# Projections over all rows in four blocks of 448 columns instead of three of 512 and one of 256, and retention values in two blocks of 384 instead of 512 and 256

## The chip, the cores and the metric

One core of a Trainium2 chip runs the whole program as a single launch. The metric is the time of one execution in microseconds on the device: the median over runs. The times before are 3032.01, 3036.05 and 3033.46 us.

## The reference

A sequence of 512 tokens, 2048 features wide, goes through one hybrid layer (dilated attention and an HGRN2 scan, then an output projection, then a gate built from a second projection) and through two further layers (retention, differential attention and an RG-LRU, then an output projection). What the change touches:

```python
# first block, once
y = concatenate([y_att, y_hg]) @ w_out            # (512, 2048) @ (2048, 2048)
h = h + rmsnorm(y, g_post)
gate = sigmoid(h @ w_pg)                          # (512, 2048) @ (2048, 2048)
e = p_l @ w_pp                                    # (512, 256) @ (256, 2048)
h = h + rmsnorm(gate * e, g_ple)
# second block, for l in range(2)
rv = (rms_norm(x) @ w_in[l])[:, 1536:2304]        # values of 6 retention heads of 128
y = concatenate([ret_out, diff_out, lru_out]) @ w_out[l]
x = x + rms_norm(y, post_norm_g[l])
```

All of it is float32. Each product is made of three matmuls on split operands: `hi*hi`, `hi*lo` and `lo*hi`, where `hi` is the value rounded to the fp32r format of TensorE and `lo` is what is left.

## The kernel before

**Projections.** `wpiece` loads a piece of weights by one DMA on SP's queue into `raw` (two buffers), ScalarE rounds it into `whi` and VectorE subtracts to get `wlo`, each in two halves (four buffers of each, so that two pieces are ready or in use). `projT` computes rows of tokens by columns of weights: for each of 16 slices `k` of 128 features and each of the four token tiles `t` it issues three matmuls whose stationary operand is a 128x128 tile of the input (`uh`, `ul`) and whose moving operand is a row of weights `cw` columns wide. With `cw=512` a piece holds two slices `k` and each `t` has a PSUM bank of its own (tile `acct`); with `cw=256` a piece holds four slices and two `t` share a bank. The callback `cb` empties a bank when its sum is complete: one `t` after the other for 512 columns, all four at the end for 256.

**Output projections.** `tok_rows` is called four times (for `w_out`, `w_pg` and `w_out_2` of both layers) and works through 2048 columns: three calls of `projT` with 512, one with 256 columns, and then a last 256 columns whose weights stay resident for all 16 slices (tile `accl`), so that the four token tiles can be finished one by one. Only when the last columns of a token tile are known can its row be normalised: `tok_rstd`, then four times `x += y * r` of 512 columns each (`SCALAR_TENSOR_TENSOR` on VectorE, tile `x`). While the last token tiles are still being multiplied, `new_rows` already transposes finished columns of `x` through a PSUM bank (tile `mb`, three banks) into the next input `uh`, `ul`. In the last layer each finished chunk is stored instead. For the gate, `ple_cols` makes `e` in column blocks: two blocks stand between the first two calls of `tok_rows`, interleaved with `new_rows` of the last two token tiles, and the other two are handed out during the second call.

**Retention.** `ret_round` runs three times per layer. Each projects `q` and `k` of two heads, rotates them (`rope`: per half, four VectorE products `rt`, one product with `C`, one addition on GpSimd), and, in rounds 0 and 2, projects values by `head_v`: four heads with `cw=512` in round 0, two with `cw=256` in round 2. The mixing of two heads (`ret_mix`) is a generator in a queue behind that of the LRU. `tick` hands out one unit of the queue each time that the projection's matmuls have earned `spacing` of credit.

**Order.** TensorE's instructions stand as they are written. The order of the other engines comes from a scheduler with priorities.

Of the kernel before, what the change touches and what calls it, by code (L numbers as in the profile page):

```python
# [17 lines left out]
P = 128  # L18
# [62 lines left out]
class Net:  # L81
# [505 lines left out]
    def head_v(self, pool, tag, wap, c0, U, h0, n, bufs=6):  # L587

        vts = []
        for h in range(0, n, 2):  # L590
            vts.append(pool.tile([P, 4, 256], F32, tag=tag, name=tag, bufs=bufs // 2))

        def vcb(t, ps):
            for h in range(n if t == 3 else 0):
                self.vts[h0 + h] = vts[h // 2][:, :, h % 2 * P:(h % 2 + 1) * P]
            for h, v in enumerate(vts):
                self.nc.scalar.activation(v[:, t, :], ps[:, h * 256:(h + 1) * 256], AF.Copy, scale=self.rc[:, t:t + 1])

        self.projT(wap, c0, U, vcb, cw=n * P)
# [188 lines left out]
    def tok_rows(self, pool, wap, gi, U, order, evac, X, fresh, before=None, more=None, at=None, src=None):  # L788
# [8 lines left out]
        V.memset(ss, EPS)  # L797
        gb = {}

        def gains(c):  # L800
            g = gb[c] = pool.tile([P, T], F32, tag="gb", name="gb", bufs=2)
            S_.dma_start(g, bass.AP(tensor=a.tensor, offset=a.offset + gi * D + c, ap=[[0, P], [1, T]]))

        def out(t, c, n, acc):
            b = c // T * T
            o = slice(c - b, c - b + n)
            i = (c + 256) // T
            ins, rest = evac(t, c, n, acc, yt[t][c // T][:, o], gb[b][:, o], ss[:, t, i:i + 1])
            if src is not None and t == 3 and i < 4:
                with self.tc.issue_after(ins.ins):  # L810
                    S_.dma_start(X[i], src[i * P:(i + 1) * P, :])
            if c == 1792:
                return rest
            rest()

        gains(0)
        for c in (0, 512, 1024):
            gains(c + 512)
            if more:
                more(c)  # L820
            self.projT(wap, c, U, lambda t, acc, c=c: out(t, c, 512, acc), range(KT) if c else order,
                       before=None if c else before)
        if more:
            more(1536)
        self.projT(wap, 1536, U, lambda t, acc: out(t, 1536, 256, acc), cw=256)
        self.drain()
        wl = []
        for i in range(0, KT, 4):
            wl.extend(self.wpiece(wap, i, 4, [1792], 256, (pool, i)))
        for t in range(4):  # L830
            acc = self.accp.tile([P, T], F32, tag="acc", name="accl")[:, 0:256]
            for i in range(KT):
                if at:
                    at(t, i)
                hi, lo = wl[i]
                uh, ul = (u[:, t * P:(t + 1) * P] for u in U[i])
                nc.tensor.matmul(acc, uh, hi, start=i == 0, stop=False)  # L837
                nc.tensor.matmul(acc, uh, lo, start=False, stop=False)  # L838
                nc.tensor.matmul(acc, ul, hi, start=False, stop=i == KT - 1)  # L839
            with self.tc.high_priority(offset=3 * BIG):  # L840
                rest = out(t, 1792, 256, acc)
                r = pool.tile([P, 2], F32, tag="r", name="r", bufs=2)
                self.tok_rstd(r[:, 1:2], r[:, 0:1], ss[:, t, :])
                rest()
                for i in ((0, 1, 2, 3) if t < 2 else (1, 2, 3, 0)):
                    x = X[t][:, i * T:(i + 1) * T]
                    V.scalar_tensor_tensor(x, yt[t][i], r[:, 1:2], x, op0=ALU.mult, op1=ALU.add)
                    fresh(t, i)

# [97 lines left out]
    def first_block(self):  # L947
# [38 lines left out]
        with tc.tile_pool(name="h1", bufs=1, reuse_waits="tile") as pool:  # L986
# [7 lines left out]

            def gated(t, c, n, acc, y, g, ss):
                ins = nc.scalar.activation(y, acc, AF.Sigmoid)
                nc.vector.tensor_tensor(y, y, es[t, c // T][:, c % T:c % T + n], op=ALU.mult)
                nc.scalar.activation(sq()[:, :n], y, AF.Square, scale=D ** -0.5, accum_out=ss)
                return ins, lambda: nc.vector.tensor_tensor(y, y, g, op=ALU.mult)

            def load(c):
                if c == 512:
                    self.tables(pool, "e", EB)
                elif c == 1024:
                    self.pT = self.load_p(pool)

            self.tok_rows(pool, A["w_out"][0], 0, U, order, self.plain(sq), X, lambda t, i: None, more=load,
                          at=self.first_half(U, X, None), src=A["x"][0])
# [12 lines left out]
            def more(c):  # L1021
                self.drain()
                if c in (512, 1024):
                    self.spacing = 6.0
                    self.add(self.ple_cols(pool, c // 512 + 1, es))

            self.tok_rows(pool, A["w_pg"][0], 1, U, range(KT), gated, X, lambda t, i: None, before, more,
                          self.first_half(U, X, self.col["pre_norm_g_2"][:, 0:16], 10))
# [4 lines left out]
    def plain(self, sq):  # L1033
        def evac(t, c, n, acc, y, g, ss):
            ins = self.nc.scalar.activation(sq()[:, :n], acc, AF.Square, scale=D ** -0.5, accum_out=ss)
            return ins, lambda: self.nc.vector.tensor_tensor(y, acc, g, op=ALU.mult)
        return evac
# [14 lines left out]
    def ple_cols(self, pool, c, es):  # L1052

        nc = self.nc
        wk = self.wpiece(self.A["w_pp"][0], 0, 2, [c * T], T)
        for t in range(4):
            ps = self.bank()
            s = slice(t * P, (t + 1) * P)
            for k in range(2):
# [3 lines left out]
                nc.tensor.matmul(ps, ul, wk[k][0], start=False, stop=k == 1)  # L1063
            es[t, c] = pool.tile([P, T], F32, tag="e", name="e", bufs=EB)
            nc.scalar.activation(es[t, c], ps, AF.Copy)
# [179 lines left out]
    def ret_round(self, pool, lp, l, r, U, C, S):  # L1245
        nc, A = self.nc, self.A
        V, S_ = nc.vector, nc.scalar
        w = A["w_in_2"][l]
        rot = self.qkv(pool, w, OFF2["rq"] + 256 * r, OFF2["rk"] + 256 * r, OFF2["rv"] + 256 * r, U, C, S, 64, 6,
                       2 * r, (4, 0, 2)[r], 6)  # L1250
        self.add(self.ret_mix(pool, lp, l, r, rot))
# [143 lines left out]
    def second_layer(self, l, U, ls8):  # L1395
# [33 lines left out]
        with tc.tile_pool(name=f"h2{l}", bufs=1, reuse_waits="tile") as pool:  # L1429
# [5 lines left out]

            def store(t, i):
                o = slice(i * T, (i + 1) * T)
                (nc.sync if i % 2 else nc.scalar).dma_start(self.out[0][t * P:(t + 1) * P, o], X[t][:, o])

            at = None if l else self.first_half(U, X, self.col["pre_norm_g_2"][:, 16:32])  # L1440
            self.tok_rows(pool, A["w_out_2"][l], 2 + l, U, order, self.plain(sq), X, store if l else lambda t, i: None,
                          at=at, src=self.xs_dram)
# [14 lines left out]
NH = 6  # L1457
EB = 8
HALF = [slice(0, T // 2), slice(T // 2, T)]
WARM = 10  # L1460
# [42 lines left out]
```

## Time and profile before

| | |
|---|---|
| median of the runs shown | 3033.46 us |
| profiled execution, its own time | 3031.51 us |
| its span, first to last instruction | 3029.7 us |
| TensorE busy | 3003.6 us, 99% of the span |
| VectorE busy | 1819.7 us, 60% |
| ScalarE busy | 1467.5 us, 48% |
| GpSimd busy | 547.1 us, 18% |
| moved by DMA | 316.25 MB, mean 104 GB/s |

The profiled execution took 1.81 us more than its span, which is what lies around the span, and 1.95 us less than the median of the runs. TensorE's instructions overlap (the next begins before the modelled end of the last), so a busy share of 99% says that there is almost always a matmul in flight; how many fit into a microsecond is read from the distance between their starts.

### The profile page before, as it was taken

What the parts mean: (1) busy time and instruction counts of PE and PEld (TensorE: products, weight loads), DVE (VectorE), ACT (ScalarE), POOL (GpSimd) and SP (SyncE); (2) the same over time, 40 slices, a digit from 0 to 9 for tenths busy, and PEclk for the clock granted to TensorE, in tenths of its full rate; (3) what the DMA queues carried; (4) which work ended last, traced back from release to release, by engine and by line L of the source; (5) the groups of instructions that cost most, each with busy time, mean ns of one, the idle gap of its engine ahead of it and who ended that gap; (6) DMA issues with size and microseconds to landing.
All of it is one profiled execution on the core that took longest, in us unless ns stands there. A gap on an engine that the chain in (4) does not pass through costs nothing. (4 is left out here: it accounts for less than half of the span.)

```text
span 3029.7 us, 40507 instructions
## 1 busy us (share of the span) xinstructions
PE 3003.6 (99%) x15118; PEld 2548.1 (84%) x15118; DVE 1819.7 (60%) x3228; ACT 1467.5 (48%) x2653; POOL 547.1 (18%) x582
## 2 busy tenths in 40 slices
PE   9999999999999999999999999999999999999998
PEld 8788888888888888889888888888988888888888
DVE  5878779557776535346766455653457664566434
ACT  6444443445556424346365544662355555446532
POOL 0546546211111000001321010110013210101000
PEclk9999999999999999999999999999999999999999
DMA  5222222333332433335332233333453322323344
GB/s 164 72 80 72 77 70 77 96 107 89 85 88 76 140 122 105 101 115 170 108 114 85 84 91 105 95 93 126 160 163 93 117 84 84 111 82 100 97 131 148
DMA packets 237878, 316.25 MB, mean 104 GB/s; under 512 B 12641, under 2 KB 179777, under 8 KB 234993
## 3 DMA queue, kind: packets, MB, share of 16 engines
q1 hardware_dynamic: 219392, 260.61, 28.0%
q0 software_dynamic: 10640, 28.92, 3.8%
q10 hardware_dynamic: 7648, 24.13, 2.4%
q8 instruction: 119, 1.95, 0.3%
q14 instruction: 79, 0.64, 0.1%
HBM read 284.25 MB, written 13.63 MB: 98 GB/s over the span
## 5 line engine op out<-in xcount | busy, mean ns | idle before, releaser
L261 DVE TENSOR_TENSOR wlo<-raw,whi 128x512 fp32r<-128x512 f32 x980 | 728.8, 754 | 741.1 <-ACT whi L260 725.2
L260 ACT ACTIVATE whi<-raw 128x512 fp32r<-128x512 f32 x980 | 604.5, 627 | 998.3 <-PE acct L321 393.0
L291 PE MATMUL acc<-uh,whi 128*128 128x512 f32 (+1 forms) x2288 | 899.1, 393 | 1.7 <-ACT whi L260 1.0
L293 PE MATMUL acc<-uh,wlo 128*128 128x512 f32 (+1 forms) x2288 | 884.5, 387 | 1.3 <-DVE wlo L261 1.3
L292 PE MATMUL acc<-ul,whi 128*128 128x512 f32 (+1 forms) x2288 | 882.6, 386 | 0.0
L319 PE MATMUL acct<-whi,uh 128*128 128x512 f32 (+1 forms) x1664 | 611.9, 368 | 3.4 <-ACT hf L534 3.4
L320 PE MATMUL acct<-wlo,uh 128*128 128x512 f32 (+1 forms) x1664 | 608.5, 366 | 0.0
L321 PE MATMUL acct<-whi,ul 128*128 128x512 f32 (+1 forms) x1664 | 608.5, 366 | 0.0
L293 PEld LDWEIGHTS acc<-uh,wlo 128*128 128x128 f32 x2288 | 430.1, 188 | 91.7 <-DVE wlo L261 3.1
L291 PEld LDWEIGHTS acc<-uh,whi 128*128 128x128 f32 x2288 | 430.7, 188 | 81.6 <-ACT whi L260 1.2
L292 PEld LDWEIGHTS acc<-ul,whi 128*128 128x128 f32 x2288 | 431.2, 188 | 79.7 <-issue 0.2
L319 PEld LDWEIGHTS acct<-whi,uh 128*128 128x128 f32 x1664 | 314.6, 189 | 54.1 <-ACT hf L534 4.2
L321 PEld LDWEIGHTS acct<-whi,ul 128*128 128x128 f32 x1664 | 314.6, 189 | 50.4
L320 PEld LDWEIGHTS acct<-wlo,uh 128*128 128x128 f32 x1664 | 314.8, 189 | 49.6 <-DVE wlo L261 0.5
L764 POOL TENSOR_TENSOR mx<-mx,gt 128x512 f32<-128x512 f32 x48 | 63.9, 1334 | 523.3 <-ACT gt L761 517.6
L853 POOL TENSOR_TENSOR r<-r,mhalf 128x1 f32<-128x1 f32 x16 | 9.1, 567 | 669.8 <-DVE r L852 669.8
L655 POOL TENSOR_TENSOR w<-w,t 128x512 f32<-128x512 f32 x56 | 78.5, 1402 | 17.4 <-DVE zz L647 17.0
L654 POOL TENSOR_TENSOR w<-w,t 128x512 f32<-128x512 f32 x56 | 70.4, 1257 | 42.6 <-DVE zz L646 42.4
L1227 POOL TENSOR_TENSOR q<-q,rt 128x512 f32<-128x512 f32 x20 | 31.8, 1588 | 244.9 <-DVE st L1361 124.0
L837 PE MATMUL accl<-whi,uh 128*128 128x256 f32 x256 | 73.1, 286 | 0.0
L838 PE MATMUL accl<-wlo,uh 128*128 128x256 f32 x256 | 71.0, 277 | 0.0
L839 PE MATMUL accl<-whi,ul 128*128 128x256 f32 x256 | 71.0, 277 | 0.0
(353 smaller groups left out, 3569.5 us busy)
## 6 DMA issues: line engine op xcount, KB each, us to landing
raw<-in_w_in SPq DMA_DIRECT2D x304, 512.0 KB
raw<-in_w_out SPq DMA_DIRECT2D x96, 512.0 KB
raw<-in_w_in SPq DMA_DIRECT2D x104, 256.0 KB
raw<-in_w_pg SPq DMA_DIRECT2D x32, 512.0 KB
x_stream<-x POOLq DMA_DIRECT2D x8, 1024.0 KB, 4.5
x<-x_stream ACTq DMA_DIRECT2D x8, 1024.0 KB
kh<-kh POOLq DMA_DIRECT2D x32, 128.0 KB, 3.0
kl<-kl POOLq DMA_DIRECT2D x32, 128.0 KB, 2.9
```

What stands on the lines that cost most here:

```text
L260: self.whis.append(nc.scalar.activation(hi, r, AF.Copy))
L261: self.wlos.append(nc.vector.tensor_tensor(lo, r, hi.bitcast(F32), op=ALU.subtract))
L291: nc.tensor.matmul(d, wk[k][0][:, s], uh, start=st, stop=False, skip_group_check=half_first)
L292: nc.tensor.matmul(d, wk[k][0][:, s], ul, start=False, stop=False, skip_group_check=half_first)
L293: nc.tensor.matmul(d, wk[k][1][:, s], uh, start=False, stop=sp, skip_group_check=half_first)
L319: nc.tensor.matmul(dst[t], uh[:, s], wk[k][0], start=st, stop=False, skip_group_check=True)
L320: nc.tensor.matmul(dst[t], uh[:, s], wk[k][1], start=False, stop=False, skip_group_check=True)
L321: nc.tensor.matmul(dst[t], ul[:, s], wk[k][0], start=False, stop=sp, skip_group_check=True)
L655: G.tensor_tensor(hv2(w1, m, 0), hv2(w1, m, 0), od.to_broadcast([P, nb, m]), op=ALU.mult)
L837: nc.tensor.matmul(acc, uh, hi, start=i == 0, stop=False)
L838: nc.tensor.matmul(acc, uh, lo, start=False, stop=False)
L839: nc.tensor.matmul(acc, ul, hi, start=False, stop=i == KT - 1)
```

## The change

`tok_rows` works in blocks of `CW = 448` columns: four calls of `projT(cw=448)` and the resident 256. With 448 columns, `projT` takes its path for wide blocks: two slices per piece, one bank per token tile. Gains, the blocks of `e` and the chunks of `x += y * r` and of the stores follow the same grid: five instead of four. `ple_cols` makes five column blocks, four of 448 and one of 256; two stand between the calls as before, three (instead of two) are handed out during the second call. The last 256 columns of `y` have a tile of their own, `yl`. `head_v` makes three heads at a time in rounds 0 and 1 (`cw=384`, two calls) instead of four in round 0 and two in round 2.

```diff
@@ head_v
-        for h in range(0, n, 2):
-            vts.append(pool.tile([P, 4, 256], F32, tag=tag, name=tag, bufs=bufs // 2))
+        g = 3 if n == 3 else 2
+        for h in range(0, n, g):
+            vts.append(pool.tile([P, 4, g * P], F32, tag=tag, name=tag, bufs=bufs // g))
@@ tok_rows
         def gains(c):
-            g = gb[c] = pool.tile([P, T], F32, tag="gb", name="gb", bufs=2)
-            S_.dma_start(g, bass.AP(tensor=a.tensor, offset=a.offset + gi * D + c, ap=[[0, P], [1, T]]))
-
-        def out(t, c, n, acc):
-            b = c // T * T
-            o = slice(c - b, c - b + n)
-            i = (c + 256) // T
-            ins, rest = evac(t, c, n, acc, yt[t][c // T][:, o], gb[b][:, o], ss[:, t, i:i + 1])
+            n = min(CW, D - c)
+            g = gb[c // CW] = pool.tile([P, CW], F32, tag="gb", name="gb", bufs=2)
+            S_.dma_start(g[:, :n], bass.AP(tensor=a.tensor, offset=a.offset + gi * D + c, ap=[[0, P], [1, n]]))
+
+        def out(t, c, acc):
+            i, n = c // CW, min(CW, D - c)
+            y = yt[t][i][:, :n] if i < 4 else pool.tile([P, D - 4 * CW], F32, tag="yl", name="yl")
+            ys[t, i] = y
+            ins, rest = evac(t, i, n, acc, y, gb[i][:, :n], ss[:, t, i:i + 1])
...
         gains(0)
-        for c in (0, 512, 1024):
-            gains(c + 512)
+        for c in range(0, 4 * CW, CW):
+            gains(c + CW)
             if more:
-                more(c)
-            self.projT(wap, c, U, lambda t, acc, c=c: out(t, c, 512, acc), range(KT) if c else order,
-                       before=None if c else before)
-        if more:
-            more(1536)
-        self.projT(wap, 1536, U, lambda t, acc: out(t, 1536, 256, acc), cw=256)
+                more(c // CW)
+            self.projT(wap, c, U, lambda t, acc, c=c: out(t, c, acc), range(KT) if c else order,
+                       cw=CW, before=None if c else before)
         self.drain()
         wl = []
         for i in range(0, KT, 4):
-            wl.extend(self.wpiece(wap, i, 4, [1792], 256, (pool, i)))
+            wl.extend(self.wpiece(wap, i, 4, [4 * CW], D - 4 * CW, (pool, i)))
...
-                for i in ((0, 1, 2, 3) if t < 2 else (1, 2, 3, 0)):
-                    x = X[t][:, i * T:(i + 1) * T]
-                    V.scalar_tensor_tensor(x, yt[t][i], r[:, 1:2], x, op0=ALU.mult, op1=ALU.add)
-                    fresh(t, i)
+                for i in ((0, 1, 2, 3, 4) if t < 2 else (1, 2, 3, 4, 0)):
+                    o = slice(i * CW, min(i * CW + CW, D))
+                    V.scalar_tensor_tensor(X[t][:, o], ys[t, i], r[:, 1:2], X[t][:, o], op0=ALU.mult, op1=ALU.add)
+                    fresh(t, o)
@@ first_block, more
-                if c in (512, 1024):
+                if c in (1, 2, 3):
                     self.spacing = 6.0
-                    self.add(self.ple_cols(pool, c // 512 + 1, es))
+                    self.add(self.ple_cols(pool, c + 1, es))
@@ ple_cols
-        wk = self.wpiece(self.A["w_pp"][0], 0, 2, [c * T], T)
+        n = min(CW, D - c * CW)
+        wk = self.wpiece(self.A["w_pp"][0], 0, 2, [c * CW], n)
         for t in range(4):
-            ps = self.bank()
+            ps = self.bank()[:, :n]
@@ ret_round
-        rot = self.qkv(pool, w, OFF2["rq"] + 256 * r, OFF2["rk"] + 256 * r, OFF2["rv"] + 256 * r, U, C, S, 64, 6,
-                       2 * r, (4, 0, 2)[r], 6)
+        rot = self.qkv(pool, w, OFF2["rq"] + 256 * r, OFF2["rk"] + 256 * r, OFF2["rv"] + 384 * r, U, C, S, 64, 6,
+                       3 * r, (3, 3, 0)[r], 6)
@@
+CW = 448
```

Three places show what the change moves. The first is VectorE in the first of the two later layers, where the first scores of retention are multiplied by their decay (`rax`) and split (`ral`). Before, the rotation of `q` of round 1 (`rt`, then `q`) stands between the LRU's scans (L1209) and `rax`:

```order
L1209 SCALAR_TENSOR_TENSOR mx_13544<-mx_13826,gi_13827 96x512
L1225 TENSOR_TENSOR rt<-q,Sr 64x512 x2
L1277 TENSOR_TENSOR rvl<-v,rvh 128x384
L261 TENSOR_TENSOR wlo<-raw,whi 128x512
L1226 TENSOR_TENSOR q<-q,Cr 128x512
L261 TENSOR_TENSOR wlo<-raw,whi 128x512
L1225 TENSOR_TENSOR rt<-q,Sr 64x512 x2
L1292 TENSOR_TENSOR rax<-mb,dec 128x512
L1226 TENSOR_TENSOR q<-q,Cr 128x512
L1294 TENSOR_TENSOR ral<-rax,rah 128x512
```

The same place in the changed kernel:

```order
L1226 TENSOR_TENSOR q<-q,Cr 128x512
L1209 SCALAR_TENSOR_TENSOR mx_13725<-mx_13977,mx_13978 96x512
L1209 SCALAR_TENSOR_TENSOR mx_13726<-mx_14005,gi_14006 96x512
L261 TENSOR_TENSOR wlo<-raw,whi 128x512
L1209 SCALAR_TENSOR_TENSOR mx_13727<-mx_14039,gi_14040 96x512
L261 TENSOR_TENSOR wlo<-raw,whi 128x512
L1292 TENSOR_TENSOR rax<-mb,dec 128x512
L1277 TENSOR_TENSOR rvl<-v,rvh 128x384
L261 TENSOR_TENSOR wlo<-raw,whi 128x384
L1294 TENSOR_TENSOR ral<-rax,rah 128x512
```

The rotation of `q` now stands before the last scans, and `rax` follows the scans after two weight splits.

The second place is ScalarE in the first call of `tok_rows`, around the end of the last streamed block: `sq,ss` empties a bank, `whi` of 128x512 here is a half piece of resident weights or of the 256-wide block. Before:

```order
L260 ACTIVATE whi<-raw 128x512 x10
L1035 ACTIVATE sq,ss<-acct 128x256
L260 ACTIVATE whi<-raw 128x512 x2
L1035 ACTIVATE sq,ss<-acct 128x256
L260 ACTIVATE whi<-raw 128x512 x2
L1035 ACTIVATE sq,ss<-acct 128x256 x2
L811 DMA x_8887<-in_x 128x2048
```

The same place in the changed kernel, where the resident halves alone are 512 wide:

```order
L260 ACTIVATE whi<-raw 128x448 x11
L260 ACTIVATE whi<-raw 128x512 x2
L260 ACTIVATE whi<-raw 128x448
L260 ACTIVATE whi<-raw 128x512 x4
L1034 ACTIVATE sq,ss<-acct 128x448 x3
L260 ACTIVATE whi<-raw 128x512 x2
L1034 ACTIVATE sq,ss<-acct 128x448
L813 DMA x_8887<-in_x 128x2048
```

The last resident piece (the pair of `whi` behind the first single `sq,ss` before, ahead of the last one now) moves from behind the first bank read to behind the third. The pairs of 128x512 after it before are the blocks of `e`.

The third place is VectorE at the end of that call, the last token tile (`x_8887`). Before:

```order
L852 TENSOR_REDUCE r<-ss 128x1
L1036 TENSOR_TENSOR mx_8967<-accl,gb 128x256
L847 SCALAR_TENSOR_TENSOR x_8887<-mx_8965,r,x_8887 128x512
L847 SCALAR_TENSOR_TENSOR x_8887<-mx_8966,r,x_8887 128x512
L847 SCALAR_TENSOR_TENSOR x_8887<-mx_8967,r,x_8887 128x512
L847 SCALAR_TENSOR_TENSOR x_8887<-mx_8964,r,x_8887 128x512
L261 TENSOR_TENSOR wlo<-raw,whi 128x512 x2
```

The same place in the changed kernel:

```order
L851 TENSOR_REDUCE r<-ss 128x1
L1035 TENSOR_TENSOR yl<-accl,gb 128x256
L846 SCALAR_TENSOR_TENSOR x_8887<-mx_8965,r,x_8887 128x448
L846 SCALAR_TENSOR_TENSOR x_8887<-mx_8966,r,x_8887 128x448
L846 SCALAR_TENSOR_TENSOR x_8887<-mx_8967,r,x_8887 128x448
L846 SCALAR_TENSOR_TENSOR x_8887<-yl,r,x_8887 128x256
L846 SCALAR_TENSOR_TENSOR x_8887<-mx_8964,r,x_8887 128x448
L261 TENSOR_TENSOR wlo<-raw,whi 128x448 x2
```

The chain has one instruction more for the same 2048 columns; the chunk that `new_rows` wants first still comes last.

## Rows read from the trace of the kernel before

**Rows 1.** The page, parts 1 and 2: busy us (share) xinstructions; granted TensorE clock in tenths.
```profile
PE 3003.6 (99%) x15118; PEld 2548.1 (84%) x15118; DVE 1819.7 (60%) x3228; ACT 1467.5 (48%) x2653; POOL 547.1 (18%) x582
...
PEclk9999999999999999999999999999999999999999
```

**Rows 2.** TensorE's groups by form: xcount | busy us, mean ns of one | idle before.
```profile
L319 PE MATMUL acct<-whi,uh 128*128 128x512 f32 x1280 | 502.9, 393 | 3.4 <-ACT hf L534 3.4
...
L319 PE MATMUL acct<-whi,uh 128*128 128x256 f32 x384 | 109.0, 284 | 0.0
...
L837 PE MATMUL accl<-whi,uh 128*128 128x256 f32 x256 | 73.1, 286 | 0.0
```

**Rows 3.** Timeline of TensorE in a 512 block, first and last of 179: start us, us.
```profile
1089.62 0.39 PE L320 MATMUL acct<-wlo,uh 128*128 128x512 f32 x1
...
1129.96 0.39 PE L321 MATMUL acct<-whi,ul 128*128 128x512 f32 x1
```

**Rows 4.** Timeline of TensorE in a 256 block, first and last of 169.
```profile
1131.78 0.28 PE L321 MATMUL acct<-whi,ul 128*128 128x256 f32 x1
...
1151.94 0.28 PE L321 MATMUL acct<-whi,ul 128*128 128x256 f32 x1
```

**Rows 5.** Timeline of TensorE, resident columns: the first, and two 100 starts apart.
```profile
1154.58 0.29 PE L837 MATMUL accl<-whi,uh 128*128 128x256 f32 x1
...
1155.62 0.28 PE L837 MATMUL accl<-whi,uh 128*128 128x256 f32 x1
...
1166.95 0.28 PE L838 MATMUL accl<-wlo,uh 128*128 128x256 f32 x1
```

**Rows 6.** Timeline of TensorE, 384-wide scores of retention and the next matmul.
```profile
2406.15 0.33 PE L1286 MATMUL mb<-rh 128*128 128x384 f32 x1
2406.32 0.34 PE L1287 MATMUL mb<-rl,rh 128*128 128x384 f32 x1
2406.50 0.34 PE L1288 MATMUL mb<-rh,rl 128*128 128x384 f32 x1
2406.67 0.39 PE L291 MATMUL acc<-uh,whi 128*128 128x512 f32 x1
```

**Rows 7.** Timeline of TensorE, first retention head of either layer: [idle before, releaser].
```profile
1591.87 0.39 PE L1307 MATMUL ro<-rah,rvh 128*128 128x512 f32 x1
1593.52 0.50 PE L1308 MATMUL ro<-ral,rvh 128*128 128x512 f32 x1 [1.26 <-DVE ral L1294]
...
2411.42 0.50 PE L1308 MATMUL ro<-ral,rvh 128*128 128x512 f32 x1 [1.25 <-DVE ral L1294]
```

**Rows 8.** Timeline of VectorE ahead of the first of these waits.
```profile
1590.27 0.69 DVE L1292 TENSOR_TENSOR rax<-mb,dec 128x512 f32<-128x512 f32 x1
1590.88 0.68 DVE L1226 TENSOR_TENSOR q<-q,Cr 128x512 f32<-128x512 f32 x1
1591.66 1.80 DVE L1294 TENSOR_TENSOR ral<-rax,rah 128x512 fp32r<-128x512 f32 x1
```

**Rows 9.** Timeline of TensorE between the first two calls of tok_rows.
```profile
1178.20 0.63 PE L863 MATMUL mb<-kc_ident,x 128*128 128x128 f32 x4 [0.90 <-DVE ul L870]
...
1181.17 0.39 PE L1061 MATMUL mb<-whi,ph 128*128 128x512 f32 x1
...
1186.67 0.60 PE L863 MATMUL mb<-kc_ident,x 128*128 128x128 f32 x4
...
1189.35 0.50 PE L1061 MATMUL mb<-whi,ph 128*128 128x512 f32 x1 [0.25 <-ACT e L1065]
...
1196.19 0.63 PE L863 MATMUL mb<-kc_ident,x 128*128 128x128 f32 x4 [0.75 <-DVE ul L870]
```

**Rows 10.** Timeline of VectorE in the same stretch.
```profile
1176.64 2.07 DVE L870 TENSOR_TENSOR ul<-mb,uh 128x256 fp32r<-128x256 f32 x6
...
1182.88 2.74 DVE L847 SCALAR_TENSOR_TENSOR x<-mx,r,x 128x512 f32<-128x512 f32 x4 [0.40 <-POOL r L853]
```

**Rows 11.** Timeline of ScalarE, the weights around the end of the 256 block.
```profile
1142.46 2.19 ACT L260 ACTIVATE whi<-raw 128x512 fp32r<-128x512 f32 x4 [4.32 <-DMA raw<-in_w_out]
...
1153.57 1.15 ACT L260 ACTIVATE whi<-raw 128x512 fp32r<-128x512 f32 x2 [1.13 <-DMA raw<-in_w_out]
```

**Rows 12.** Timeline of VectorE: the last resident piece, and the end of the program.
```profile
1154.23 1.29 DVE L261 TENSOR_TENSOR wlo<-raw,whi 128x512 fp32r<-128x512 f32 x2 [1.34 <-ACT whi L260]
...
3023.14 2.74 DVE L847 SCALAR_TENSOR_TENSOR x<-mx,r,x 128x512 f32<-128x512 f32 x4 [0.40 <-POOL r L853]
```

## What was predicted

> **What bounds the kernel now.** I read the page's first two parts first: TensorE is busy for 99% of the span at the full granted clock [rows 1], so time can only come from the distance between the starts of its matmuls and from the few waits in its stream. Then the groups by form: the wide blocks of the output projections and values are 1280 matmuls of 512 and 384 of 256 columns per product, the resident columns 256 of 256, all three products alike, and the one idle time shown for them (3.4 us) lies at the start of the kernel, which the change does not touch [rows 2]. The durations in that view overlap and are no price; the distance of starts is, and the timeline gives it.
>
> In a 512 block, 179 starts lie between 1089.62 and 1129.96 us: 40.34 us over 178 steps, 226.6 ns each [rows 3]. In a 256 block, 168 steps take 20.16 us: 120.0 ns each [rows 4]. The 384-wide scores of retention take 0.52 us for three, 173.3 ns each [rows 6]. At the clock's upper level of 2.4 GHz 512, 384 and 256 columns are 213.3, 160.0 and 106.7 ns, so each of the three carries the same 13.3 ns on top. The resident columns alone run closer: 100 steps in 11.33 us, 113.3 ns, or 6.7 ns on top [rows 5].
>
> **The change part by part.**
>
> *Matmuls of the output projections.* For each feature slice, token tile and product, before has three matmuls of 512 and one of 256, the new kernel four of 448; the resident one stays. That is four against four, with 1792 columns either way. No row shows 448 columns. Between its neighbours at 384 and 512 a straight line gives 173.3 + (226.6 - 173.3)/2 = 200.0 ns, and 4 x 200.0 = 800.0 stands against 3 x 226.6 + 120.0 = 799.8. With 16 slices x 4 tiles x 3 products x 4 calls = 768 such sets the difference is +0.2 us at the resolution of the rows: zero. The bounds: if 512's rate per column held (0.4427 ns) 448 would cost 198.3 ns; if 448 were charged as 512, 226.6. I take 200.0, because three measured widths lie on one line.
>
> *Matmuls of the values.* 226.6 + 120.0 = 346.6 becomes 2 x 173.3 = 346.6 ns, 192 times per layer: zero.
>
> *Blocks of e.* 96 matmuls of 512 become 96 of 448 and 24 of 256: 96 x 200.0 + 24 x 120.0 - 96 x 226.6 = +0.3 us. But the first 48 stand between two calls of `tok_rows`, where TensorE covers other engines: these alone shrink by 48 x 26.6 = 1.3 us. The first 24 (from 1181.17 to 1186.67) cover VectorE's last chain `x += y * r`, which ends at 1182.88 + 2.74 = 1185.62 [rows 9, 10]. Its cover of 1.05 us shrinks by 24 x 26.6 = 0.64 us and holds. The next 24 alternate with transposes and already wait for ScalarE's copy of `e` and VectorE's `ul` (0.25 and 0.75 us) [rows 9], so part of the other 0.64 us comes back as waiting. Bounds +0.3 to +1.6, taken +0.6.
>
> *One more instruction in each chain `x += y * r`.* Four of 512 in a row take 2.74 us, 685 ns each, six of 256 take 2.07, 345 ns each [rows 10]: twice the columns, twice the time, so a fifth instruction costs nothing back to back. The upper bound: one operation alone takes 0.69 [rows 8], two of that width in a row 1.29 us [rows 12], so 0.1 us is at stake where a neighbour does not hide it. Such a chain sets the end at five places: before the transposes that wait 0.90 us for `ul` behind it [rows 9] (once in each of three calls), between the calls, and at the program's end, where the last chain runs from 3023.14 to 3025.88 behind the last matmul and only stores follow [rows 12]. Five times 0 to 0.1, taken +0.25 in all. The other chains lie beside matmuls. Gains and stores are five DMAs instead of four, on ScalarE's and SP's queues; the last store is the smaller one of 448 columns, priced at nothing.
>
> *The wait in retention.* In either layer TensorE stands 1.25 us before the first `ral` matmul, with 1.65 us between starts where 0.23 would do [rows 7]. It waits for VectorE, which made `rax` only at 1590.27 and `ral` at 1591.66, with the second product of `q`'s rotation between [rows 8]. That rotation came late because the projection of `q` of round 1 ended just as the first scores were multiplied. Round 0 now makes 384 instead of 512 columns of values: 192 x 53.3 ns = 10.2 us less. So that projection ends some 10 us earlier against the same credit, while the queue hands out the first score at about the same place; the order shows the rotation ahead of the last scans. VectorE has the same work ahead of `rax` though, and can only use the gaps that it left. If none is used, the wait stays; if all goes, 1.25 plus the slow start behind it is 1.4 us per layer. I take 1.2 per layer, as `ral` no longer shares its time with the rotation (1.80 us there for an operation that takes 0.69 elsewhere in these rows): -2.4, bounds -2.8 and 0. Round 1's values now follow `k` and carry the mixing that round 2's did; a new meeting of the rotation with a score would cost the same 1.4 us.
>
> *Weights.* A call makes 36 pieces instead of 32 on SP's queue, 448 KB instead of 512 for the wide ones, and 8 conversions more on ScalarE and VectorE; the values 16 of 384 KB per layer instead of 12. A piece of 448 lasts TensorE 24 x 200 = 4.8 us and is loaded and split beside it; these two engines are busy 48% and 60% [rows 1]. What may come late is the last resident piece. Before, the last streamed piece was split from 1142.46 on, 12.1 us ahead of the first resident matmul at 1154.58 [rows 5, 11], which is about two pieces of 48 x 120.0 = 5.76 us; the last resident piece, held by its DMA, was ready at 1154.23 + 1.29 = 1155.52 [rows 12]. It is first needed after 36 matmuls, at 1154.58 + 36 x 0.1133 = 1158.66: 3.1 us to spare. Two pieces of 448 last 9.6 instead of 11.5 us, so the whole train moves 1.9 us later and 1.2 us remain. ScalarE reads three banks ahead of it, which is over in time. Price zero, and what it costs without that cover is a rival.
>
> *Sum:* 0 + 0 + 0.6 + 0.25 - 2.4 = -1.55 us on the profiled execution's 3031.51 us, which lies 1.95 us below the median of the runs. On the median: 3033.46 - 1.55 = **3031.9 us**. A measurement of this kernel can tell about 0.2%, 6.1 us, from no change.
>
> **The rivals.**
>
> *A floor under the 256 blocks.* If 512's 0.4427 ns per column is the true rate, and 256 columns cost 120.0 instead of 113.3 ns because something else ends later, then 448 costs 198.3 and 384 170.0 ns. That saves 768 x (799.8 - 793.2) + 384 x (346.6 - 340.0) = 5.1 + 2.5 = 7.6 us: 3024.3 us. For it speaks that the resident 256 columns do run at 113.3 [rows 5]; against it the 384-wide matmuls at 173.3 [rows 6], three in a row only. Chance 0.12. The Trainium skill (TensorE: Matmul & The Clock Gate, sections "LDWEIGHTS" and "Back-to-back issue gap") gives such a floor: loading 128 stationary columns takes 128/1.2 = 106.7 ns, and the spacing of a stream is set by load and matmul together. By that rule an estimated 106.7 ns of load stands level with 256 columns, and blocks of 448 would hide it where 256 could not; the trace agrees only so far as 256 is never closer than 113 ns.
>
> *A closer stream.* If 448 and 384 settled into the spacing of the resident columns, 6.7 ns on top, 3072 + 768 matmuls would save 6.7 ns each: 25.6 us, 3006.3 us. In 178 steps of 512 nothing like it shows. Chance 0.05.
>
> *The last resident piece is late* (slower). Its place is the first token tile of the resident columns, slices 12 to 15, four times. It decides once it comes 1.9 us beyond the 1.2 us of cover, since four times 1.9 less 1.55 is 6.1 us. At 2.5 us each: +10 - 1.55, 3041.9 us. For it speaks that `x`'s load of 1 MB now starts as the 448 block ends instead of behind the 256 block's four reads, beside that piece; against it that its DMA is issued before. Chance 0.07.
>
> *448 charged as 512* (slower): 3072 x 26.6 ns = 81.7 us, 3113.6. Widths that are multiples of 128 are all that was measured. Chance 0.04.
>
> *The wait in retention only moves:* 3034.3 us or, with one more of 1.4 us in each layer, 3037. No change that can be told, and part of the forecast's case.
>
> **How the numbers follow.** Forecast case 0.66, the rivals 0.12, 0.05, 0.07 and 0.04, and 0.06 for waits or gains not seen here (0.04 slower, 0.02 faster). Faster: 0.12 + 0.05 + 0.02 = 0.19. Same: 0.66. Slower: 0.07 + 0.04 + 0.04 = 0.15. The likeliest case alone runs from 3029 (both waits gone wholly, nothing lost to `e`, less the scatter of a median of three, 1.45 us below it here) to 3037. The range reaches to the floor rival below, 3023.5, and up to small lateness of the resident piece, 3040; the closer stream, 512's charge and the late piece in full, 0.16, and part of the unseen stay outside.
>
> **What would show it.** Starts 200.0 ns apart in 448 blocks and 173.3 in the values' (198.3 and 170.0 would be the floor rival); the resident columns still at 113.3; no wait of TensorE for `ral` in the first retention head; no wait for `whi` or `wlo` in the first resident token tile; the waits between the two calls within 1 us of before. I am wrong if 448 is off the line, or if a split arrives late where the pieces became shorter.

## The result, and the profile after

The changed kernel takes 3057.60 us (median of 4 runs, 3055.56 to 3061.42) against 3032.74 us of the kernel before on the same chip (4 runs, 3030.09 to 3036.05): a ratio of 1.0086, interval 1.0074 to 1.0098. The ratios here and below are those on record, estimated from all runs; the plain quotient of two medians differs from them by up to 0.0004 (here it is 1.0082). It is slower by some 25 us, outside the predicted range. The profiled execution after is the 3061.42 us one, the slowest of the four; 1.8 us of its length arise in the first 80 us, where the program is the same, so stretches are compared and not only ends.

The page after, parts 1 and 2, as in [rows 1]:
```profile
PE 3025.4 (99%) x15142; PEld 2621.9 (86%) x15142; DVE 1832.3 (60%) x3294; ACT 1476.0 (48%) x2699; POOL 549.4 (18%) x582
...
PEclk9999999999999999999999999999999999999999
```
The clock is the same and TensorE is still never idle for long, so matmuls stand further apart or wait briefly. TensorE's groups by form, as in [rows 2]:
```profile
L319 PE MATMUL acct<-whi,uh 128*128 128x448 f32 x1024 | 375.5, 367 | 0.4 <-DVE gt L761 0.4
...
L319 PE MATMUL acct<-whi,uh 128*128 128x384 f32 x256 | 86.0, 336 | 0.0
...
L836 PE MATMUL accl<-whi,uh 128*128 128x256 f32 x256 | 73.9, 289 | 0.0
```
The durations tell nothing, as before; the distance of starts does. The timeline of TensorE in two blocks of 448 columns, each time the first and last of 52 starts (what [rows 3] showed for 512):
```profile
1143.35 0.37 PE L319 MATMUL acct<-whi,uh 128*128 128x448 f32 x1
...
1153.89 0.37 PE L319 MATMUL acct<-whi,uh 128*128 128x448 f32 x1
...
2149.65 0.36 PE L321 MATMUL acct<-whi,ul 128*128 128x448 f32 x1
...
2159.99 0.36 PE L321 MATMUL acct<-whi,ul 128*128 128x448 f32 x1
```
51 steps take 10.54 us in the first call and 10.34 us in the third: 206.7 and 202.7 ns, not the forecast 200.0. These are two settled states. In the first every step is 206 or 207 ns, in the second they go 199, 207, 202, 203, 202 and again. In these traces a stream keeps its state until something interrupts it. The values' 384 columns, 34 starts:
```profile
1560.04 0.33 PE L319 MATMUL acct<-whi,uh 128*128 128x384 f32 x1
...
1565.76 0.33 PE L319 MATMUL acct<-whi,uh 128*128 128x384 f32 x1
```
33 steps in 5.72 us are 173.3 ns, as in [rows 6].

The rest lies in waits at the end of each call of `tok_rows`. TensorE's waits in the stretches of resident columns, call 1, call 2 (two) and call 3, in square brackets the idle time and what ended it:
```profile
1180.50 0.55 PE L862 MATMUL mb<-kc_ident,x 128*128 128x128 f32 x3 [3.42 <-DVE x L846]
...
1396.54 0.55 PE L862 MATMUL mb<-kc_ident,x 128*128 128x128 f32 x3 [1.65 <-DVE x L846]
...
1405.88 0.63 PE L862 MATMUL mb<-kc_ident,x 128*128 128x128 f32 x4 [1.81 <-DVE ul L873]
...
2230.89 0.63 PE L862 MATMUL mb<-kc_ident,x 128*128 128x128 f32 x4 [1.31 <-DVE ul L873]
```
The transposes of the new rows wait for the chains `x += y*r` (before: no such wait) and for the `ul` behind them. Before, the second kind is shorter, in calls 2 and 3:
```profile
1386.81 0.63 PE L863 MATMUL mb<-kc_ident,x 128*128 128x128 f32 x4 [1.15 <-DVE ul L874]
...
2204.76 0.63 PE L863 MATMUL mb<-kc_ident,x 128*128 128x128 f32 x4 [0.29 <-DVE ul L874]
```
For the first of the waits after, that of 3.42 us, the timeline of ScalarE and then of VectorE:
```profile
1164.45 0.33 ACTq L813 DMA_DIRECT2D x<-in_x  x1
...
1166.81 0.58 ACT L260 ACTIVATE whi<-raw 128x448 fp32r<-128x448 f32 x1 [0.80 <-DMA raw<-in_w_pp]
...
1174.47 1.05 ACT L260 ACTIVATE whi<-raw 128x448 fp32r<-128x448 f32 x2 [5.09 <-DMA raw<-in_w_pp]
1175.42 0.36 ACT L1034 ACTIVATE sq<-accl 128x256 f32<-128x256 f32 x1
```
```profile
1165.00 1.29 DVE L261 TENSOR_TENSOR wlo<-raw,whi 128x512 fp32r<-128x512 f32 x2 [1.10 <-ACT whi L260]
...
1169.49 0.42 DVE L1035 TENSOR_TENSOR yl<-accl,gb 128x256 f32<-128x256 f32 x1
1175.08 0.63 DVE L261 TENSOR_TENSOR wlo<-raw,whi 128x448 fp32r<-128x448 f32 x1 [5.17 <-ACT whi L260]
1175.62 2.47 DVE L846 SCALAR_TENSOR_TENSOR x<-mx,r,x 128x448 f32<-128x448 f32 x4
1178.01 0.48 DVE L846 SCALAR_TENSOR_TENSOR x<-yl,r,x 128x256 f32<-128x256 f32 x1
```
Rows 0 were ready for their chain at 1169.9, but the split of the second `e` piece (`w_pp`) stands ahead of it on VectorE, and ahead of the read of rows 1 on ScalarE. Its transfer landed only at 1174.5. A load of 1 MB of `x` had been asked for at 1164.45; that the one delays the other is tested below. That one late piece holds 5.2 us of VectorE, and TensorE 3.4.

I cut each profiled execution into stretches by the starts of TensorE's instructions. Microseconds for the kernel before, and what each other one takes more (the other kernels are those of the next section):
```
              before  after  x_early  held_448  widths_5454  held_5454  values_alone
to call 1    1000.62  +3.00    +0.77     +1.46        -1.23      +1.23         +1.12
blocks 1      153.96  +5.61    +2.82     +2.64        +0.19      +0.70         +0.17
resident 1     26.59  +5.33    +0.62     +0.70        +0.65      +0.34          0.00
e, blocks 2   181.10  +3.57    +4.46     +4.47        +0.81      +0.84         -0.03
resident 2     26.85  +3.02    +3.02     +1.94        +3.97      +2.50         +0.01
layer 1       639.00  +1.64    +2.28     +1.45        +0.66      +1.26         +0.39
blocks 3      153.64  +2.48    +2.48     +2.48        +0.12      +0.18         +0.02
resident 3     25.98  +1.49    +1.68     +1.49        +1.71      +1.48          0.00
layer 2       638.28  +1.70    +1.72     +1.93        +1.96      +1.80         +1.93
blocks 4      153.69  +2.42    +2.43     +2.43        +0.07      +0.13         -0.03
resident 4     21.94  -0.01    +0.83     +0.83        +0.04      +0.10          0.00
tail            8.08  -0.33    -0.33     -0.32        -0.16      -0.15         -0.02
```
After: the four block stretches +14.1 us, the resident stretches +9.8, the layers with the values +3.3, the unchanged start +3.0. The size of the waits differs from run to run: in the trace of the blocks alone (next section) the blocks take 12.0 us more and the resident stretches 8.8, of which call 1 has 2.7 instead of 5.3.

### The profile page after: what moved, and what is told of

Same layout as the page of the kernel before. It is cut to its first block, busy times and chain, and to the rows that moved or that the text cites. A ratio compares the mean times of both kernels' runs of the same rounds, so it can differ in the third digit from the quotient of the medians.

```text
span 3059.6 us, 40812 instructions
## 1 busy us (share of the span) xinstructions
PE 3025.4 (99%) x15142; PEld 2621.9 (86%) x15142; DVE 1832.3 (60%) x3294; ACT 1476.0 (48%) x2699; POOL 549.4 (18%) x582
## 4 chain that ended last, share of the span: by engine, by line
PE 85%; DVE 5%; issue 4%; DMA 3%; ACT 3%; POOL 1%; ACTq 0%; SPq 0%; DVEq 0%; POOLq 0%
PE acc L291 15%; PE acc L293 15%; PE acc L292 15%; PE acct L319 10%; PE acct L320 10%; PE acct L321 10%; PE mb L680 1%; DVE wlo L261 1%; DMA raw<-in_w_in 1%; PE mb L498 1%; DVE x L846 1%; PE do L1387 1%; DMA raw<-in_w_out 1%; PE accl L837 1%; PE accl L836 1%
## 5 line engine op out<-in xcount | busy, mean ns | idle before, releaser
L261 DVE TENSOR_TENSOR wlo<-raw,whi 128x512 fp32r<-128x512 f32 (+2 forms) x1030 | 749.3, 738 | 771.4 <-ACT whi L260 748.8
L260 ACT ACTIVATE whi<-raw 128x512 fp32r<-128x512 f32 (+2 forms) x1030 | 614.4, 607 | 1044.8 <-PE acct L321 444.7
L319 PE MATMUL acct<-whi,uh 128*128 128x448 f32 (+2 forms) x1664 | 615.1, 370 | 3.8 <-ACT hf L534 3.4
L320 PE MATMUL acct<-wlo,uh 128*128 128x448 f32 (+2 forms) x1664 | 611.8, 368 | 0.3 <-DVE wlo L261 0.3
L321 PE MATMUL acct<-whi,ul 128*128 128x448 f32 (+2 forms) x1664 | 611.4, 367 | 0.0
```

The costliest lines, as they stand in the source:

```text
L260: self.whis.append(nc.scalar.activation(hi, r, AF.Copy))
L261: self.wlos.append(nc.vector.tensor_tensor(lo, r, hi.bitcast(F32), op=ALU.subtract))
L319: nc.tensor.matmul(dst[t], uh[:, s], wk[k][0], start=st, stop=False, skip_group_check=True)
L320: nc.tensor.matmul(dst[t], uh[:, s], wk[k][1], start=False, stop=False, skip_group_check=True)
L321: nc.tensor.matmul(dst[t], ul[:, s], wk[k][0], start=False, stop=sp, skip_group_check=True)
```

## The experiments

**The two halves of the change**, each alone. `values_alone` is the kernel before with the new `head_v` and this edit; `blocks_alone` is the changed kernel with both undone.
```diff
-        rot = self.qkv(pool, w, OFF2["rq"] + 256 * r, OFF2["rk"] + 256 * r, OFF2["rv"] + 256 * r, U, C, S, 64, 6,
-                       2 * r, (4, 0, 2)[r], 6)
+        rot = self.qkv(pool, w, OFF2["rq"] + 256 * r, OFF2["rk"] + 256 * r, OFF2["rv"] + 384 * r, U, C, S, 64, 6,
+                       3 * r, (3, 3, 0)[r], 6)
```


> The kernel before with one part of the change, the retention values in two blocks of 384. Spacing theory (the loss is made in the token-row blocks: 3072 matmuls of 448 columns start 204.8 ns apart on the mean instead of the forecast 200.0, +14.8 us, and the waits of the new blocks add some 10): this half costs nothing, between -2.4 us (the wait for ral goes) and +1 us (the waits for wlo, 0.92 us each, that stand in its place after the change). Values theory (rival: the wider blocks of 384 delay what follows in the retention rounds): +5 us or more.

> The changed kernel with the retention values as before, so the four blocks of 448 alone. Spacing theory: the whole loss, +23 to +28 us against the kernel before. Values theory: under +20 us.

Measured: the values alone 3032.91 us against 3032.44, ratio 1.0001 (0.9992 to 1.0010); the blocks alone 3058.45, ratio 1.0083 (1.0070 to 1.0097). The whole loss is in the blocks; the values theory fell. In the trace of the values alone the wait for `ral` [rows 7] is gone and another stands in its place, in either layer:
```profile
1586.11 0.50 PE L293 MATMUL acc<-uh,wlo 128*128 128x512 f32 x1 [0.75 <-DVE wlo L261]
...
2405.98 0.50 PE L293 MATMUL acc<-uh,wlo 128*128 128x512 f32 x1 [0.76 <-DVE wlo L261]
```

**Other widths on the same grid.** Four blocks of 512, 384, 512 and 384 columns, the same number of instructions in each stage.
```diff
-CW = 448
+CB = (0, 512, 896, 1408, 1792, 2048)
...
-                       cw=CW, before=None if c else before)
+                       cw=CB[b + 1] - CB[b], before=None if b else before)
```


> The changed kernel with blocks of 512, 384, 512 and 384 columns in place of four of 448 (same columns in all, same four blocks, same resident 256, same e blocks by that grid, retention values 384). Spacing theory: 512 and 384 columns start 226.6 and 173.3 ns apart as in the kernel before, so the 14.8 us come back: at most +10 us against the kernel before, all of it waits. Grid theory (rival: four blocks of other edges, with the weights, x and e pieces arriving at other moments, make the loss, and the wide spacing is only how waiting shows in the records): +20 us or more, as with 448.

Measured: 3041.44 us, ratio 1.0028 (1.0017 to 1.0039): +9.0, where 448 has +25. The block stretches are back within 0.2 us of before, 0.8 in call 2, and 12.9 us below those of 448. So most of the loss, some 16 of 25 us, hangs on the widths of the blocks and not on their number. The +9.0 that is left is taken up below.

**The spacing by itself.**
```diff
+for name, w, n in SECTIONS:
...
+    for i in range(n):
+        hi, lo = wk[i % 2]
+        for t in range(4):
+            s = slice(t * P, (t + 1) * P)
+            d = acc[t][:, :w]
+            nc.tensor.matmul(d, uh[:, s], hi[:, :w], start=i == 0, stop=False)
+            nc.tensor.matmul(d, uh[:, s], lo[:, :w], start=False, stop=False)
+            nc.tensor.matmul(d, ul[:, s], hi[:, :w], start=False, stop=i == n - 1)
```


> Leaves out the whole computation: after one load and six copies TensorE runs groups of three matmuls as in the projections (new weights each time, accumulating in four banks) at one width after the other from 512 down to 256 columns, then 448 again three times, behind other widths. Nothing is loaded or waited for. Spacing theory: 448 columns start 202.7 to 206.7 ns apart here too, while 512, 384 and 256 show 226.6, 173.3 and 120.0; other widths that are no multiple of 128 may be off the line as well. Grid theory: 448 columns start 200.0 ns apart when nothing waits, and every width lies on the line of 384 and 512 (0.4167 ns a column plus 13.3 ns).

> Leaves out the whole computation, as the first run of widths. More widths, and at 448 columns one thing changed at a time: accumulators at column 64 of the bank, operands at column 64 of their tile, 64 weight columns instead of 128, 64 rows of contraction instead of 128, the same tile for all three weights, and longer stretches behind 512, 384 and 256 columns. If the spacing belongs to the width alone, all these 448 stay at 202.7 or 206.7 ns. If it comes of the weight load (188 ns long in the trace, about as long as 448 columns take), half the weight columns or rows give 200.0. If it comes of where a tile lies, the shifted ones change.

Measured in the first: timeline of TensorE, the first and last row of a section of 400 columns (96 matmuls) and two rows 180 starts apart in the last section of 448:
```profile
173.57 0.35 PE L1500 MATMUL a<-r,r 128*128 128x400 f32 x1
...
190.67 0.34 PE L1502 MATMUL a<-r,r 128*128 128x400 f32 x1
...
359.08 0.37 PE L1501 MATMUL d<-r,r 128*128 128x448 f32 x1
...
396.29 0.37 PE L1501 MATMUL d<-r,r 128*128 128x448 f32 x1
```
95 steps in 17.10 us are 180.0 ns, on the line through 384 and 512. 180 steps in 37.21 us are 206.7 ns, with nothing loaded or waited for. In the same way for each width of the two runs (one execution of each), mean ns of a step, and ns above that line (0.4167 ns a column and 13.3):
```
columns  256   272   288   304   320   336   352   368   384   392   400   408   416
ns     120.0 126.6 131.7 137.8 146.7 153.4 161.1 166.7 173.4 177.3 180.0 185.0 188.3
above    0.0   0.0  -1.6  -2.2   0.0   0.1   1.1   0.1   0.1   0.7   0.0   1.7   1.7

columns  424   432   440   448          456   464   472   480   488   496   504   512
ns     190.0 195.8 200.0 202.7, 206.7 208.8 209.9 213.3 216.6 220.0 223.3 226.7 226.7
above    0.0   2.5   3.3   2.7,   6.7   5.5   3.3   3.3   3.3   3.3   3.3   3.4   0.0
```
So both states of 448 appear without any of the kernel's surroundings, and the spacing theory holds. In the second run the 448 columns stay at 202.7 with the accumulators or the operands moved by 64 columns and with one tile for all weights. With 64 rows of contraction they settle at 206.7. With 64 weight columns (tile `f`) they settle at 202.2, although the weight load (PEld, the last number but one is the mean ns of one) falls from 188 to 134 ns:
```profile
L1505 PEld LDWEIGHTS d<-r,r 128*128 128x128 f32 x32 | 6.0, 188 | 0.5
...
L1505 PEld LDWEIGHTS f<-r,r 128*64 128x64 f32 x32 | 4.3, 133 | 2.1
```
The first and the last of the 96 starts of these matmuls:
```profile
367.43 0.37 PE L1504 MATMUL f<-r,r 128*64 128x448 f32 x1
...
386.64 0.37 PE L1506 MATMUL f<-r,r 128*64 128x448 f32 x1
```
Neither the place of a tile nor the weight load makes it; it belongs to the width. Why these widths stand off the line, no run here shows. The state after an interruption is open: behind 512 columns the stream settled at 202.7 in both runs, behind 384 at 206.7 in both, behind 256 at 202.7.

**The last load of x earlier**, beside that of the third row block, in the changed kernel:
```diff
-            if src is not None and t == 3 and i < 4:
+            if src is not None and t == 3 and i < 3:
...
-                    S_.dma_start(X[i], src[i * P:(i + 1) * P, :])
+                    for j in (i, 3)[:1 + i // 2]:
+                        S_.dma_start(X[j], src[j * P:(j + 1) * P, :])
```


> The changed kernel with the last 1 MB of x (or of the kept rows) asked for at the end of the third block, beside the third, instead of at the end of the fourth, where its transfer runs beside the first e weights. Collision theory: the 3.4 to 3.6 us for which the transposes of the new rows wait at the end of the first call (1176.81 us after the change) fall to the 1.1 us that the kernel before waits there, so -2 to -3 us in all. Rival (the second e piece is late because the four blocks hand back their weight buffers later, x has nothing to do with it): that wait stays over 3 us and the time within 1 us.

Measured: 3055.95 us, ratio 1.0078 (1.0064 to 1.0092). The wait of 3.4 us is gone, and the resident stretch of call 1 is 4.7 us shorter than after the change (+0.62). ScalarE's timeline, the same split:
```profile
1165.26 1.05 ACT L260 ACTIVATE whi<-raw 128x448 fp32r<-128x448 f32 x2 [2.40 <-DMA raw<-in_w_pp]
```
It ends before the read of rows 1, and the collision theory holds for its place. Against the kernel before the loss is +23.8 us instead of +24.9: this gain of 1.1 us is under the 2 to 3 expected, and the runs do not resolve it. The waits of call 2 are untouched: nothing is loaded into `x` there.

**Both new waits at the other widths.** In the kernel of 512 and 384 columns, the load moved as above, and the last block's 256 values of rows 1 and 3 in places of their own, instead of all four rows in one buffer:
```diff
-            y = yt[t][i][:, :n] if i < 4 else pool.tile([P, n], F32, tag="yl", name="yl")
+            y = yt[t][i][:, :n] if i < 4 else yo[t // 2] if t % 2 else pool.tile([P, n], F32, tag="yl", name="yl")
...
+        yb = self.cp.tile([P, T], F32, name="rb")
+        yo.extend((yb[:, 0:256], yb[:, 256:512]))
```


> The kernel with blocks of 512, 384, 512 and 384 columns, with the earlier last load as in the run with the changed kernel, and with a second home for the last block's 256 values (rows 1 and 3 no longer wait for the buffer of rows 0 and 2; SBUF has no room for more of the old kind, so the scale buffer lends its own). If the +9 us that were left at these widths are the two new waits at the rows' ends (late e weights and one buffer for the last block): the second call's wait of 2.4 us for x falls under 1 us, and the time lies within 0 to +6 us of the kernel before. If the waits are made by the fourth block's own evacuation and the fifth instruction of the chain: +8 to +10 us, as without these edits.

Measured: 3043.20 us, ratio 1.0037 (1.0024 to 1.0050), no gain. In call 1 these widths had no wait for `x` (resident stretch +0.65), so the moved load had nothing to take away there. TensorE in call 2 of `widths_5454` and of this kernel:
```profile
1380.92 0.55 PE L862 MATMUL mb<-kc_ident,x 128*128 128x128 f32 x3 [2.38 <-DVE x L846]
```
```profile
1382.66 0.55 PE L865 MATMUL mb<-kc_ident,x 128*128 128x128 f32 x3 [1.87 <-DVE x L849]
```
My theory for this wait fell. ScalarE in `widths_5454` shows what I had passed over:
```profile
1370.78 1.16 ACT L260 ACTIVATE whi<-raw 128x512 fp32r<-128x512 f32 x2 [2.52 <-DMA raw<-in_w_in]
1371.84 0.37 ACT L995 ACTIVATE yl<-accl 128x256 f32<-128x256 f32 x1
```
The read of rows 0 stands behind the split of a piece for the next stage (`w_in`) that has not landed. It looks like the mechanism of call 1 without the load of `x`; the next runs test that.

**The splits held back.** Nothing but the order on ScalarE and VectorE: those splits follow the reads and chains that they had stood before.
```diff
+        self.held = [[], [rd[1], ch[4]]] if gi == 0 else [[rd[0]], [rd[0], ch[4]]] if gi == 1 else []
...
+            held = [] if keep or not self.held else self.held.pop(0)
...
+                    for x in held[:1]:
+                        st.enter_context(self.tc.issue_after(x.ins))
```


> The changed kernel, in which the splits of the second e piece stay behind ScalarE's read of the last block for rows 1 and VectorE's chain of rows 0 (first call), and those of the first two pieces of w_in behind the last square of rows 0 (second call). Nothing else is moved. Queue theory (a late piece's split stands ahead of the end of rows 0 on ScalarE and VectorE, and so makes the new rows late): the waits of 3.58 and 1.81 us before the transposes at 1176.81 and 1394.62 us go, the resident stretch of call 1 comes to within 2 us of the kernel before (it was 5.3 us longer) and that of call 2 to within 2 us (it was 3.0 us longer); the time falls by 3 to 6 us from the changed kernel's, to +19 to +22 us against the kernel before. Rival (the waits come of the last block's own wider evacuation): the waits stay over 1.5 us and the time within 1.5 us of the changed kernel's.

> The same edit in the kernel with blocks of 512, 384, 512 and 384 columns. Queue theory: the 2.55 us wait of the second call goes under 1 us, the resident stretch of call 2 comes to within 2 us of the kernel before (it was 4.0 us longer), and the time falls from +9 us to +5 to +7 us against the kernel before. Rival: +8 us or more. Either way no gain over the kernel before: no wait of before is taken away but that for ral.

Measured: with 448 columns 3053.24 us against 3031.71, ratio 1.0068 (1.0054 to 1.0081): +21.5, 3.3 us less than the change's +24.9; the intervals overlap a little, so the stretches decide. TensorE in call 2 of this kernel:
```profile
1387.20 0.55 PE L871 MATMUL mb<-kc_ident,x 128*128 128x128 f32 x3 [0.56 <-DVE x L854]
...
1396.55 0.63 PE L871 MATMUL mb<-kc_ident,x 128*128 128x128 f32 x4 [1.80 <-DVE ul L882]
```
The wait for `x` falls from 1.65 to 0.56 us, that of call 1 is gone, and the two stretches stand at +0.70 and +1.94. The queue theory holds. At the other widths the wait falls from 2.38 to 0.62 us and the stretch of call 2 from +3.97 to +2.50, short of the 2 expected. TensorE in call 2:
```profile
1369.89 0.38 PE L844 MATMUL accl<-whi,uh 128*128 128x256 f32 x1 [0.27 <-ACT whi L264]
...
1370.66 0.39 PE L845 MATMUL accl<-wlo,uh 128*128 128x256 f32 x1 [0.38 <-DVE wlo L268]
...
1382.15 0.55 PE L871 MATMUL mb<-kc_ident,x 128*128 128x128 f32 x3 [0.62 <-DVE x L854]
```
The first two are waits for the last resident piece, which `widths_5454` has too (0.31 and 0.38) and 448 does not. The time does not follow: 3041.67 us, ratio 1.0030 (1.0019 to 1.0042), against 1.0028 without the edit, as the rival said. The trace has 2.0 us less in the resident stretches than that of `widths_5454`, but 2.5 more in the start, where the two programs are the same, and 1.1 more in blocks and layers. At these widths the order is shown to set the wait, and not shown to set the time. No version here beats the kernel before.

## Why the prediction was wrong

**Matmuls of the output projections: the step that failed.** "I take 200.0, because three measured widths lie on one line." They do, and so do 320, 400 and 424 among others in the experiment, but 448 does not: 202.7 or 206.7 ns, 2.7 or 6.7 above. Over 3072 matmuls the settled steps of the changed kernel come to 12.5 us more than at 200.0 each, most of the +14.1 in its block stretches, and to 10.0 to 10.9 in the three other traces with 448 columns, where less of the first call ran at 206.7. The prediction named it ("I am wrong if 448 is off the line") and its bounds, 198.3 to 226.6, held the value. But the upper bound entered the forecast only as a rival at its far end, chance 0.04. Nothing between 200.0 and 226.6 had a chance, and the upper end of the range was set by another rival, the late resident piece. At 1 ns each 3072 matmuls make 3.1 us; 2 ns of doubt are already the 6.1 us that can be told from no change.

**The floor rival** would have needed 198.3 ns. The weight load is 188 ns long in these streams, and with 64 weight columns, at 134 ns, the spacing of 448 columns fell only from 202.7 to 202.2 ns, so the load is not what sets it. The Trainium skill (TensorE: Matmul & The Clock Gate, section "LDWEIGHTS") gives a load the time of its columns divided by 1.2, by which an estimate for 128 columns is 106.7 ns. The records here are some 81 ns longer; they agree only in what the second 64 columns add, 54 ns where the same division gives an estimated 53.

**Weights: the second step that failed.** "Price zero", it said. The lag itself was read rightly: the last resident piece is ready at 1166.29 us (VectorE's row of 1165.00 above), 3.10 us behind the first resident matmul instead of 0.94, so 2.2 us later where 1.9 was forecast. That is still 1.0 us ahead of the matmul that needs it; the two rows of TensorE:
```profile
1163.19 0.28 PE L836 MATMUL accl<-whi,uh 128*128 128x256 f32 x1
...
1167.29 0.28 PE L836 MATMUL accl<-whi,uh 128*128 128x256 f32 x1
```
I stopped at that piece. The next ones in the same train, for `e` in call 1 and for `w_in` in call 2, slip as well; they have ample time by their own use, but their splits are queued ahead of the reads that end the last block. That `x`'s load would run "beside that piece" was foreseen for the wrong piece. The resident stretches of calls 1 and 2 cost 8.4 us in the trace after and 6.3 in that of the blocks alone; with the order alone changed 2.6 are left.

**One more instruction in each chain: mis-sized.** Forecast +0.25 for five places, at most 0.1 each. Four of 448 and one of 256 run from 1175.62 to 1178.49, 2.87 us instead of 2.74. But TensorE's wait for the `ul` behind the chain of rows 2 grows from 1.15 to 1.81 us in call 2 and from 0.29 to 1.31 in call 3, more than the chain. The wait of call 3 is 1.29 to 1.31 us in every trace whose chain has five chunks, of 448 or of 512 and 384 columns, so it goes with the grid and not with the 448. What makes up the rest beyond the chain (it may be the order of the evacuation ahead of it) was not tested and stays open.

**The wait in retention: it moved.** The wait for `ral` went, as forecast, but not the 2.4 us: a wait for `wlo` of 0.75 us stands in its place, and some tenths more at the end of the values for their copy on ScalarE (0.18 us at 1566.62 after the change). The rival "only moves" was right, and the values alone measure 1.0001. Their trace has +2.3 us in the two layers, less than those runs resolve.

**The values' matmuls** came as forecast, 173.3 ns. **The blocks of e** cost less than forecast, about 0.1 us where 0.6 was taken and 0.3 was the lower bound: from the last resident matmul of call 1 to the first block of call 2 the changed kernel takes 1.4 us less, and the matmuls of `e` within call 2 take 1.5 more. So next to nothing of the first came back as waiting.

## What to carry to other kernels

Do not take the spacing of a matmul stream at a width that no row shows from a line through others: measure it with a stream of that width alone, or cut at widths that are measured, here 384 and 512, whose blocks cost nothing more (the kernel cut so is 9 us slower all the same, mostly for its waits). When a train of loads slips, follow it past the first consumer: a split that is early for its own use can still stand on its engine ahead of something that is due. And where thousands of equal instructions change, give the nanosecond its own term and range.

## What the runs showed of the hardware

The step between matmuls, with new weights for each, is not smooth in the number of columns. 256, 384, 400 and 512 lie on one line, 288 and 304 lie 1.6 and 2.2 ns below it, and each of the widths from 464 to 504 lies 3.3 or 3.4 ns above it, so that 504 columns take 226.7 ns, as 512 do. At 448 columns a stream has two stable spacings, 202.7 and 206.7 ns, at the same granted clock (1.00 in both). An interruption can move it from one to the other: in the changed kernel at 1021 us, behind two longer steps, and at 1257 and 1346 us, behind six matmuls of `e`. The weight load, 188 ns long, can shrink to 134 with the step at 448 columns only 0.5 ns shorter.
